# A hybrid encoder layer on one core: the scan's diagonal products with x stationary, and a step planner with other costs

## The chip, the cores and the metric

The kernel runs on one core of a Trainium2 chip, in one launch. The metric is the device time of an execution in microseconds (us). Its engines are named as in the profile: PE (TensorE, the matmuls), PEld (its weight loads), DVE (VectorE), ACT (ScalarE), POOL (GpSimd) and SP (SyncE, whose queue issues the transfers). A matmul has a stationary operand, loaded into the array, and a moving one, streamed through it. [...]

## The reference

One encoder layer is applied to two sequences, 1024 and 256 tokens long, with the same weights: `x + W_out @ concat(scan, window attention, memory attention)(RMSNorm(x))`. The scan group has 16 heads of 64 channels in two groups of eight, chunks of 128 tokens, and runs in both directions over the sequence. What matters here is the part inside a chunk:

```python
seg = acs[:, :, :, None] - acs[:, :, None, :]
decay = jnp.exp(jnp.where(tril, seg, -jnp.inf))
cb = jnp.einsum('bcign,bcjgn->bcijg', Cm, Bm)
y_diag = jnp.einsum('bcijgr,bcjgrp->bcigrp', cb[..., None] * decay, xdt)
...
y = (y_f + y_b + d_skip[:, None] * xs).reshape(b, T, SSD_WIDTH)
```

For each chunk and head, `y_diag` is a product of a 128x128 matrix of weights (positions against positions) with the chunk's 128x64 values. Everything is f32.

## The kernel before, in words

The 1280 tokens are ten blocks of 128. The kernel works in f32 accuracy by splitting each operand of the large projections into a high and a low part in the one-pass type f32r and doing three products. The names: `wh`, `wl` are the weights' parts (made by ACT and DVE from the loaded `wraw`), `xH`, `xL` those of the rows, `acc` the PSUM tiles of the projections (five banks). All other work uses the pool `mix`, three PSUM banks.

The first 740 us of the program and the last 350 are projections with little beside them. In between, the projections to keys, queries, gates and the first half of the output go on, and the scan and both attentions run beside them in four lanes (`ATT`, `SSD`, `PREP`, `DEC`). Each lane is a queue of generators. A generator yields in front of each small step and says with `wants(tiles, banks, after)` which tiles the step needs, how many PSUM banks of `mix` it will open, and which other steps must have been written. `pump`, called after each group of three projection products of a block, gives each lane credit and takes the first lane, in a fixed order, whose next step `may` go.

Whether it may is decided by `Clocks`, a planner that runs while the program is written and not on the chip. It holds a time for each engine, a time at which each tile is full and one at which it is free. `Clocks.cost` estimates an instruction (in ns, `n` elements a partition), `Clocks.ran` moves the clocks on, and `Clocks.ready` compares a step's wants with PE's clock. So an estimate that is off moves a step in each engine's order. On the chip every engine then works through its own order and waits at an instruction whose input is not there. Transfers all go through SP's queue.

The steps around the change are in `decay(t)`, in the lane `DEC`, for each block `t`. Letters stand for them: `R` loads rows of cumulative decay (`rf` and `rb`, by DMA from `ac`), `E` adds a bias on ACT, `C` chooses between the directions on DVE, `D` takes exponentials on ACT, `W` multiplies by `cb` on DVE, which gives the weights `mt` (in the tile `rb`). `Y`, the function `diag(g)`, forms the eight products of group `g` into the bank `py`: the stationary operand is `mt` of one head, 128 columns, and the moving one is that head's 64 columns of `x` (the tile `xs`). DVE then multiplies `x` by the skip and diagonal coefficients into `sk`, adds it to `ya`, adds `py`, and SP stores `ya`. There are 20 such sets, two for each block, with 160 products.

Other names that appear below: `po`, the value products of the window attention (64 columns of `v_all` stationary, two key heads side by side in the output's partitions); `pr`, the four transposes that turn the scan's normalised rows; `psc`, `nm`, `lg` and `ppt`, the window attention's scores, their maxima, their exponentials and the turning of these; `qss`, `qr` and `q`, the norm of the queries (a sum of squares on DVE, a power on POOL, a multiply on DVE); `pmt`, `mpT`, `pmq`, `mqh`, `pms` and `moT`, tiles of the memory attention; `pst`, the scan's state; `xc`, `pxs`, the scan's channels and their turning; `pcb`, the products that give `cb`.

Of the kernel before, what the change touches and what calls it, by code (L numbers as in the profile page):

```python
# [10 lines left out]
F32 = mybir.dt.float32  # L11
# [4 lines left out]
AF = mybir.ActivationFunctionType  # L16
# [3 lines left out]
P = 128  # L20
# [10 lines left out]

RATES = {'kv': (4, 4), 'mq0': (8, 8), 'z0': (8, 8), 'z1': (8, 8), 'mq1': (8, 8), 'o': (8, 8)}
DEBT = 6.0
AHEAD, QUEUE = 300.0, 4000.0
NEG = -1e30

UNITS = (0, 4, 1, 5, 2, 6, 7, 3, 8, 9)
# [5 lines left out]
class Clocks:  # L43
# [17 lines left out]
    def cost(self, e, ins, ops, power):  # L61
        n = max([self.size(x) for x in ops] or [1])
        if e == "PE":
            m = self.size(ops[0])
            one_pass = ops[-1].dtype == F32R or ops[1].dtype == F32R
            return m / 2.4 + 14 if one_pass else max(m / 0.6, 213) + 6
        if e == "DVE":
            return 150 + 1.05 * n
        if e == "ACT":
            return (190 + 0.8 * n if n > 16 else 190) + (190 if len(ins.outs) > 1 else 0)  # L70
        if e == "POOL":
            return 60 + 4.2 * n if n > 16 else 250 + 180 * n if power else 300
        return 50

    def ran(self, e, ins, power=False):
        outs, srcs = [[x.bass_ap for x in xs if hasattr(x, "bass_ap")] for xs in (ins.outs, ins.ins)]
        cost = self.cost(e, ins, outs + srcs, power)
        if e != "SP":
            self.now[e] = max(self.now[e], self.now["PE"])
        if not self.lane:  # L80
            self.now[e] += cost
            return
        at = self.now[e] if e != "SP" else self.now["PE"]
        for x in srcs:
            at = max(at, self.full.get(self.name(x), 0.0))
        for x in outs:
            at = max(at, self.free.get(self.name(x), 0.0))
        if e == "SP":
            end = at + 2600 + self.size(outs[0]) * 1.5
        else:  # L90
            end = self.now[e] = at + cost + 20
        for x in srcs:
            k = self.name(x)
            self.free[k] = max(self.free.get(k, 0.0), end)
        for x in outs:
            k = self.name(x)
            if e != "SP":
                self.free[k] = max(self.free.get(k, 0.0), end)
            self.full[k] = end + 90
# [10 lines left out]

    def ready(self, want):
        tiles, n = want[:2]
        at = [self.full.get(self.name(x), 0.0) - (0 if n else AHEAD) for x in tiles]
        at += [self.opens("mix", 3, i + 1) - 400 * i for i in range(n)]
        at += [self.now[e] - QUEUE for e in ("ACT", "DVE")]
        return max(at) <= self.now["PE"]

# [28 lines left out]
def wants(*tiles, banks=0, after=()):  # L146
    return tiles, banks, after
# [3 lines left out]
def hymba_encoder_kernel(  # L151
# [8 lines left out]
    V, A, G, T, S = [Timed(clk, n, e) for n, e in (("DVE", nc.vector), ("ACT", nc.scalar), ("POOL", nc.gpsimd),  # L160
                                                  ("PE", nc.tensor), ("SP", nc.sync))]
# [18 lines left out]
    fin = early.enter_context(tc.tile_pool(name="early", bufs=1))  # L180
    acc = ctx.enter_context(tc.tile_pool(name="acc", bufs=5, space=bass.MemoryType.PSUM))
    mix = ctx.enter_context(tc.tile_pool(name="mix", bufs=3, space=bass.MemoryType.PSUM))
# [5 lines left out]
    def const(shape, name, dtype=F32):  # L188
        return cp.tile(shape, dtype, tag=name, name=name)
# [4 lines left out]
    def psum(name):  # L194
        return mix.tile([P, 512], F32, tag="mix", name=name)
# [3 lines left out]
    ident = identr.bitcast(F32)  # L199
# [9 lines left out]


    rx = const([P, 14], "rx")
    rbc = const([P, 640], "rbc")
    gq = const([P, 64], "gq")
    dskip, sinkb, dtb, aneg = const([P, 16], "dskip"), const([P, 8], "sinkb"), const([P, 32], "dtb"), const([P, 32], "aneg")
    nsink, pow8 = const([P, 8], "nsink"), const([P, 8], "pow8")
    for h in range(8):
        G.memset(pow8[:, h:h + 1], 2.0 ** (h + 1))
    carry = fin.tile([P, 12, 4], F32, tag="carry", name="carry")
    def dram(shape, name):
        return dr.tile(shape, F32, tag=name, name=name)  # L220
# [32 lines left out]
    ATT, SSD, PREP, DEC = range(4)  # L253
    wanted = [None] * 4
    turn = [0]
    said = set()
# [40 lines left out]
    def may(i):  # L297
        w = wanted[i]
        return owed[i] >= 1 and lanes[i] and (w is None or (said.issuperset(w[2]) and clk.ready(w)))

    def pump(rates):

        for i in range(4):
            owed[i] = min(owed[i] + rates[i % 2], DEBT) if lanes[i] else 0.0
        while True:
            i = next((j for j in (ATT, PREP, SSD, DEC) if may(j)), None)
            if i is None:
                return
            owed[i] -= 1
            step(i)  # L310
# [631 lines left out]
    xs_of, cb_of, dco_of, ya_of = {}, {}, {}, {}  # L942
# [113 lines left out]
    def decay(t):  # L1056
# [4 lines left out]
        def rows(q):  # L1061

            rf = mp.tile([P, 512], F32, tag="rf", name="rf", bufs=2)
            mt = mp.tile([P, 512], F32, tag="rb", name="rb", bufs=RBB)
            r0 = 32 * (t % 5) + 4 * q
            for d, r in enumerate((rf, mt)):
                S.dma_start(r, ac_d[t // 5][r0 + 16 * d:r0 + 16 * d + 4, :]
                            .rearrange("h c -> (h c)").partition_broadcast(P))
            rows_[q] = rf, mt
# [25 lines left out]
        def diag(g):  # L1095
            py = psum("py")
            x, a = xs_of[t][g], ya_of[t, g]
            for h in range(8):
                mt = mts[2 * g + h // 4]
                T.matmul(py[:, h * 64:h * 64 + 64], mt[:, (h % 4) * P:(h % 4 + 1) * P],  # L1100
                         x[:, h * 64:h * 64 + 64], start=True, stop=True)
            sk = a if first else mp.tile([P, 512], F32, tag="rf", name="sk", bufs=2)
            V.tensor_mul(hv(sk), hv(x), hb(dco_of[t][:, 8 * g:8 * g + 8], 8, 64))
            if not first:
                V.tensor_add(a, a, sk)
            V.tensor_add(a, a, py)
            S.dma_start(yp_d[t][:, g * 512:(g + 1) * 512], a)

        rows(0)
        rows(1)  # L1110
        cbs = (("ssd_one", t, "cb"),)
        for what, q in [(x[0], int(x[1])) for x in "E0 C0 E1 D0 R2 C1 W0 D1 E2 W1 C2 Y0 R3 D2 E3 W2 C3 D3 W3".split()]:
            if what == "R":
                rows(q)
            elif what == "E":
                yield wants(rows_[q][0])
                expo(q)
            elif what == "C":
                yield wants(*rows_[q])
                choose(q)  # L1120
            elif what == "D":
                yield wants(rows_[q][1])
                decays(q)
            elif what == "W":
                yield wants(rows_[q][1], after=cbs)
                weights(q)
            else:
                yield wants(mts[1], mts[0], banks=1, after=(("ssd_one", t, 0),))
                diag(0)
        said.add(("decay", t, "weighed"))  # L1130
        yield wants(mts[3], banks=1, after=(("ssd_one", t, 1),))
        diag(1)


    last_y = {}
# [123 lines left out]
    for k in range(8):  # L1259
        at = 2 * k - 5 if k < 4 else 4 * k - 13 if k < 7 else 13  # L1260
# [612 lines left out]
```

## Time and profile before

| | us |
|---|---|
| median of 3 runs | 1775.78 |
| lowest and highest | 1773.38, 1777.44 |
| the profiled execution | 1773.83 |
| its span in the trace | 1772.1 |

The profile is of that one execution. Its rows of matmuls give a start and a duration, and durations of successive matmuls overlap, so that the cost of one in a stream is the distance between starts. An f32 product is recorded as two matmuls, a transpose or an f32r product as one; a few records may be missing. In a row of the timeline stand the start, the duration of the group in us, engine, line, operation, output <- inputs, the stationary shape as rows*columns, the output's shape and the number of records, and in brackets the idle time of that engine just before and what ended it. In a row of the waits stand who waited, for whom, the total in us, how often, and the longest.

### The profile page before, as it was taken

Reading aid. Unit: us, or ns where it says so; the run is one execution under the profiler, and the core shown is the slowest. Engines: PE = TensorE matmul, PEld = TensorE weight load, DVE = VectorE, ACT = ScalarE, POOL = GpSimd, SP = SyncE. Lnnn points to the kernel's source line nnn. Section 1 sums busy time; section 2 is a strip of 40 time slices with the busy share of each in tenths; the row PEclk is TensorE's granted clock in tenths of the full one; section 3 lists DMA queues with packets and bytes.
Section 4 is the critical chain, followed back from the end, with each engine's and each line's share of the span. In section 5 each row is a group of like instructions: output and inputs, shape, how many; then the busy total and the mean of one; then the engine's idle time right before and its main releaser. Section 6 shows DMA issues by size and latency. Waiting matters only on the chain.

```text
span 1772.1 us, 30974 instructions
## 1 busy us (share of the span) xinstructions
PE 1755.3 (99%) x10306; PEld 1572.0 (89%) x10306; DVE 1310.9 (74%) x2417; ACT 971.8 (55%) x2181; POOL 683.8 (39%) x1092
## 2 busy tenths in 40 slices
PE   9999999999999999999999999999999999999999
PEld 7889999999899999988788877887788888889999
DVE  5596788989968888797777877678776533766665
ACT  6554555445545444346787666658886532433332
POOL 0026798860478989220110000111200100068775
PEclk9999999999999999999999999999999999999999
DMA  8794454446544333376467766767785734644442
GB/s 293 238 319 175 136 149 148 128 143 194 156 119 145 119 104 106 90 216 208 143 188 249 259 213 192 226 190 230 243 249 161 222 110 147 207 142 147 145 144 77
DMA packets 210993, 313.23 MB, mean 177 GB/s; under 512 B 21584, under 2 KB 84368, under 8 KB 210832
## 3 DMA queue, kind: packets, MB, share of 16 engines
q1 hardware_dynamic: 210688, 311.19, 56.7%
q8 instruction: 81, 1.33, 0.3%
q14 instruction: 80, 0.66, 0.1%
q10 hardware_dynamic: 144, 0.06, 0.0%
HBM read 242.42 MB, written 68.75 MB: 176 GB/s over the span
## 4 chain that ended last, share of the span: by engine, by line
PE 88%; DMA 4%; DVE 3%; ACT 2%; issue 1%; POOL 1%; SPq 0%; ACTq 0%; DVEq 0%; POOLq 0%
PE acc L128 66%; PE accm L128 11%; PE py L128 2%; PE po L128 1%; PE psc L128 1%; PE pst L128 1%; PE pmo L128 1%; PE pms L128 1%; PE ppt L128 1%; DMA wraw<-in_w_in_laid_dram 1%; PE pyf L128 1%; DMA xst<-in_x_prompt_dram 1%; DVE wl L128 1%; PE pyb L128 0%; ACT lg L128 0%
## 5 line engine op out<-in xcount | busy, mean ns | idle before, releaser
L128 PE MATMUL acc<-wh,xH 128*128 128x512 f32 (+1 forms) x1248 | 490.0, 393 | 0.1
L128 DVE TENSOR_TENSOR wl<-wraw,wh 128x512 fp32r<-128x512 f32 (+1 forms) x480 | 355.5, 744 | 172.9 <-ACT wh L128 170.1
L128 PE MATMUL acc<-wl,xH 128*128 128x512 f32 (+1 forms) x1248 | 473.7, 380 | 0.7 <-DVE wl L128 0.5
L128 PE MATMUL acc<-wh,xL 128*128 128x512 f32 (+1 forms) x1248 | 472.1, 378 | 0.0
L128 ACT ACTIVATE wh<-wraw 128x512 fp32r<-128x512 f32 (+1 forms) x480 | 291.5, 613 | 211.6 <-PE acc L128 136.5
L128 POOL TENSOR_TENSOR ws<-wraw 128x128 f32<-128x128 f32 x224 | 156.9, 700 | 365.8 <-DMA wraw<-in_w_in_pairs_dram 163.1
L128 PEld LDWEIGHTS acc<-wl,xH 128*128 128x128 f32 x1248 | 234.7, 188 | 45.1 <-issue 6.5
L128 PEld LDWEIGHTS acc<-wh,xH 128*128 128x128 f32 x1248 | 234.6, 188 | 44.9 <-issue 7.0
L128 PEld LDWEIGHTS acc<-wh,xL 128*128 128x128 f32 x1248 | 234.2, 188 | 44.6 <-issue 1.0
L128 ACT ACTIVATE sh<-ws 128x384 fp32r<-128x384 f32 x224 | 115.5, 522 | 253.3 <-POOL ws L128 126.6
L128 DVE TENSOR_TENSOR sl<-ws,sh 128x384 fp32r<-128x384 f32 x224 | 158.7, 712 | 115.4 <-ACT sh L128 113.9
L128 POOL TENSOR_TENSOR ws<-wraw,ws 128x128 f32<-128x128 f32 x224 | 153.1, 683 | 17.2
L128 POOL TENSOR_TENSOR ws<-ws,wraw 128x128 f32<-128x128 f32 x224 | 154.3, 689 | 0.0
L128 POOL TENSOR_TENSOR wraw<-wraw 128x128 f32<-128x128 f32 x224 | 139.8, 624 | 17.1
L128 PE MATMUL acc<-xH,wl 128*128 128x320 f32 x320 | 100.0, 312 | 1.0 <-DVE wl L128 1.0
L128 PE MATMUL acc<-tH,sl 128*128 128x320 f32 x320 | 98.9, 309 | 0.0
L128 PE MATMUL acc<-xL,wh 128*128 128x320 f32 x320 | 98.9, 309 | 0.0
L128 PE MATMUL accm<-tH,wl 128*128 128x320 f32 x320 | 98.8, 309 | 0.0
L128 PE MATMUL acc<-tH,sh 128*128 128x320 f32 x320 | 98.7, 309 | 0.0
L128 PE MATMUL acc<-xH,wh 128*128 128x320 f32 x320 | 98.7, 309 | 0.0
L128 PE MATMUL accm<-tL,wh 128*128 128x320 f32 x320 | 98.5, 308 | 0.0
L128 PE MATMUL accm<-tH,wh 128*128 128x320 f32 x320 | 98.5, 308 | 0.0
(458 smaller groups left out, 3829.1 us busy)
## 6 DMA issues: line engine op xcount, KB each, us to landing
wraw<-in_w_in_pairs_dram SPq DMA_DIRECT2D x160, 256.0 KB, 2.7
wraw<-in_w_in_laid_dram SPq DMA_DIRECT2D x128, 256.0 KB, 3.6
wraw<-in_w_out_laid_dram SPq DMA_DIRECT2D x64, 256.0 KB, 3.1
wraw<-in_w_out_pairs_dram SPq DMA_DIRECT2D x64, 256.0 KB, 2.9
rf<-ac SPq DMA_DIRECT2D x40, 256.0 KB, 3.8
rb<-ac SPq DMA_DIRECT2D x40, 256.0 KB, 4.2
wraw<-in_w_mem_laid_dram SPq DMA_DIRECT2D x32, 256.0 KB, 4.7
ra<-in_x_turned_dram SPq DMA_DIRECT2D x16, 320.0 KB, 3.8
```

The costliest lines, as they stand in the source:

```text
L128: r = f(*a, **kw)
```

## The change

Three things change. The diagonal products swap their operands: the 64 columns of `x` of one head are stationary, the weights `mt` are moving, the output has 64 partitions, and an even and an odd head stand side by side in the 128 partitions of `py`, which now holds the result turned. ACT copies it to a new tile `yT`, and a new step `T`, the function `back(g)`, turns it with four transposes into a second bank `pyt`, from which DVE adds. The planner's costs and rules change: estimates for all engines, a latency after ACT and DVE (`LATE`), a margin for tiles that a PE step needs and for banks in place of a fixed advance of 300 ns, and another order of the lanes from the last memory attention of the first half until the sixth block of the scan's second pass. And the row `rbc` of the norm's factors moves to the pool that is given back before the lanes begin.

```diff
-AHEAD, QUEUE = 300.0, 4000.0
+MARGIN, QUEUE = {"PE": 700.0, "bank": 300.0, "other": 0.0}, 4000.0
+LATE = {"ACT": 110.0, "DVE": 90.0}
...
-            return m / 2.4 + 14 if one_pass else max(m / 0.6, 213) + 6
+            return max(m / 2.4 + 14, 85) if one_pass else max(m / 0.6, 213) * list(ops[0].ap)[0][1] / 128 + 6
         if e == "DVE":
-            return 150 + 1.05 * n
+            return 67 + 1.04 * n
         if e == "ACT":
-            return (190 + 0.8 * n if n > 16 else 190) + (190 if len(ins.outs) > 1 else 0)
+            aps = sum(hasattr(x, "bass_ap") for x in ins.ins)
+            return (50 if ops[-aps].space == "PSUM" else 92) + 0.835 * n + 92 * (aps - 1) + (92 if len(ins.outs) > 1 else 0)
         if e == "POOL":
             return 60 + 4.2 * n if n > 16 else 250 + 180 * n if power else 300
...
-            end = self.now[e] = at + cost + 20
+            self.now[e] = at + cost
+            end = at + cost + LATE.get(e, 20)
...
-        at = [self.full.get(self.name(x), 0.0) - (0 if n else AHEAD) for x in tiles]
-        at += [self.opens("mix", 3, i + 1) - 400 * i for i in range(n)]
+        at = [self.full.get(self.name(x), 0.0) + MARGIN["PE" if n else "other"] for x in tiles]
+        at += [self.opens("mix", 3, i + 1) - 400 * i + MARGIN["bank"] for i in range(n)]
...
-    rbc = const([P, 640], "rbc")
+    rbc = fin.tile([P, 640], F32, tag="rbc", name="rbc")
...
-            i = next((j for j in (ATT, PREP, SSD, DEC) if may(j)), None)
+            late = ("mem_attn", 4) in said and ("ssd_two", 5) not in said
+            i = next((j for j in ((SSD, DEC, ATT, PREP) if late else (ATT, PREP, SSD, DEC)) if may(j)), None)
...
                 mt = mts[2 * g + h // 4]
-                T.matmul(py[:, h * 64:h * 64 + 64], mt[:, (h % 4) * P:(h % 4 + 1) * P],
-                         x[:, h * 64:h * 64 + 64], start=True, stop=True)
+                o = h % 2 * 64
+                T.matmul(py[o:o + 64, h // 2 * P:(h // 2 + 1) * P], x[:, h * 64:h * 64 + 64],
+                         mt[:, (h % 4) * P:(h % 4 + 1) * P], start=True, stop=True)
+            yT = mp.tile([P, 512], F32, tag="yT", name="yT", bufs=1)
+            A.activation(yT, py, AF.Copy)
+            yT_.append(yT)
+
+        def back(g):
+            x, a = xs_of[t][g], ya_of[t, g]
+            yT = yT_.pop()
+            py = psum("pyt")
+            for j in range(4):
+                T.transpose(py[:, j * P:(j + 1) * P], yT[:, j * P:(j + 1) * P], ident)
             sk = a if first else mp.tile([P, 512], F32, tag="rf", name="sk", bufs=2)
...
-        for what, q in [(x[0], int(x[1])) for x in "E0 C0 E1 D0 R2 C1 W0 D1 E2 W1 C2 Y0 R3 D2 E3 W2 C3 D3 W3".split()]:
+        for what, q in [(x[0], int(x[1])) for x in "E0 C0 E1 D0 R2 C1 W0 D1 E2 W1 C2 Y0 R3 D2 E3 T0 W2 C3 D3 W3".split()]:
...
         diag(1)
+        yield wants(yT_[0], banks=1)
+        back(1)
```

How the order on the engines moves is shown at three places. The first is PE at the first set of diagonal products, of the last block of the long sequence. Before:

```order
L128 MATMUL acc<-wh,xH_5674 128x512
L128 MATMUL acc<-wl,xH_5674 128x512
L128 MATMUL acc<-wh,xL_5675 128x512
L128 MATMUL py<-xs,rb 128x64 x8
L128 MATMUL acc<-wh,xH_5674 128x512
L128 MATMUL acc<-wl,xH_5674 128x512
L128 MATMUL acc<-wh,xL_5675 128x512
```

And now, from the products on:

```order
L131 MATMUL py<-rb,xs 64x128 x8
L131 MATMUL acc<-wh,xH_5580 128x512
L131 MATMUL acc<-wl,xH_5580 128x512
L131 MATMUL acc<-wh,xL_5581 128x512
L131 MATMUL acc<-wh,xH_5580 128x512
L131 MATMUL acc<-wl,xH_5580 128x512
L131 MATMUL acc<-wh,xL_5581 128x512
```

The products have 64 output partitions and 128 columns in place of 128 and 64, and stand 18 projection products earlier; their transposes `pyt` follow 15 projection products later.

The second is PE at the twelfth set, in the third block from the front of the long sequence. Before:

```order
L128 MATMUL pst<-bh,bth 128x512
L128 MATMUL pst<-bl,bth 128x512
L128 MATMUL pst<-bh,btl 128x512
L128 MATMUL acc<-wh,xH_12222 128x512
L128 MATMUL acc<-wl,xH_12222 128x512
L128 MATMUL acc<-wh,xL_12223 128x512
L128 MATMUL py<-xs,rb 128x64 x8
L128 MATMUL ppt<-identr,lg 128x128 x6
```

And now:

```order
L131 MATMUL pcb<-bc 128x128
L131 MATMUL pcb<-identr,bc 128x128
L131 MATMUL py<-rb,xs 64x128 x8
L131 MATMUL pmt<-identr,mpr 128x128 x4
L131 MATMUL acc<-wh,xH_12729 128x512
L131 MATMUL acc<-wl,xH_12729 128x512
L131 MATMUL acc<-wh,xL_12730 128x512
L131 MATMUL pyt<-identr,yT 128x128 x4
L131 MATMUL pxs<-identr,xc 128x128 x8
```

Here the transposes follow the products closely, behind the turning of the memory attention's weights and three projection products.

The third is DVE at the queries of the second block, where its multiply waits for POOL's power. Before:

```order
L128 TENSOR_REDUCE qss<-sq 128x8
L128 ISA lg,nm<-psc,ndist,nsink 128x256
L128 ISA nm 128x1
L128 TENSOR_TENSOR wl<-wraw,wh 128x512
L128 TENSOR_TENSOR q<-q,qr 128x512
L128 COPY_PREDICATED rb<-upper,rf 128x512
L128 TENSOR_TENSOR qh<-q,qh 128x4x64
L128 ISA lg,nm<-psc,ndist,nsink 128x256
```

And now:

```order
L131 COPY_PREDICATED rb<-upper,rf 128x512
L131 TENSOR_REDUCE qss<-sq 128x8
L131 TENSOR_TENSOR wl<-wraw,wh 128x512
L131 TENSOR_TENSOR q<-q,qr 128x512
L131 ISA lg,nm<-psc,ndist,nsink 128x256
L131 ISA nm 128x1
```

Between the sum of squares and the multiply stood a score step of two instructions and a split; now only the split stands there.

More of the change, by code (lines that the diff above doesn't have):

```diff
@@ L1107, in diag @@
             S.dma_start(yp_d[t][:, g * 512:(g + 1) * 512], a)
+        yT_ = []
         rows(0)
@@ L1132, in decay @@
         diag(1)
+        yield wants(yT_[0], banks=1)
+        back(1)
     last_y = {}
```

4 lines of the change are left out of this document (3 added, 1 removed).

## The prediction

> **What bounds the kernel now.** I read the head of the page first, then the chain of waits.
>
> ```profile
> span 1772.1 us, 30974 instructions
> PE 1755.3 (99%) x10306; PEld 1572.0 (89%) x10306; DVE 1310.9 (74%) x2417; ACT 971.8 (55%) x2181; POOL 683.8 (39%) x1092
> PE 88%; DMA 4%; DVE 3%; ACT 2%; issue 1%; POOL 1%; SPq 0%; ACTq 0%; DVEq 0%; POOLq 0%
> ```
>
> TensorE sets the end: 99% busy, and 88% of the chain. So there are two ways to gain, less work on PE or less of the 1% in which it waits. Busy time is no measure of the first, because each record's duration has a tail that lies over the next record. I therefore read starts from the timeline. For the second, the busy time by stretch, over the part in which the scan and the attention run beside the projections:
>
> ```profile
> core 0: us, PE busy (x) PEld busy (x) DVE busy (x) ACT busy (x) POOL busy (x), PEclk, DMA share, GB/s
> 740.00:800.00 60.00, 58.84 (x344) 51.55 (x343) 52.27 (x130) 27.24 (x63) 9.67 (x16) 1.00 0.63 184
> 800.00:950.00 150.00, 147.94 (x808) 121.22 (x808) 118.62 (x274) 111.15 (x316) 17.91 (x32) 1.00 0.61 190
> 950.00:1100.00 150.00, 146.53 (x802) 118.17 (x799) 112.00 (x244) 102.98 (x275) 11.55 (x21) 1.00 0.70 223
> 1100.00:1250.00 150.00, 148.20 (x813) 120.28 (x812) 113.97 (x249) 102.38 (x261) 22.23 (x45) 1.00 0.71 224
> 1250.00:1420.00 170.00, 168.70 (x939) 137.32 (x938) 114.04 (x258) 118.76 (x321) 19.10 (x40) 1.00 0.70 213
> ```
>
> Of these 680 us PE is busy for 670.2: it waits for 9.8 us, and the clock is full throughout. DVE is busy for 511 us of them (75%), ACT for 463 (68%). The waits one by one, the longest first:
>
> ```profile
> PE py L128 <- ACT mpT L128: 2.3, 1, 2.3
> PE ppt L128 <- DVE nm L128: 1.4, 1, 1.4
> PE po L128 <- ACT pT L128: 0.9, 1, 0.9
> PE pms L128 <- DVE mql L128: 0.9, 1, 0.9
> PE pxs L128 <- DMA xc<-xbc_d: 0.8, 1, 0.8
> ```
>
> The change hardly touches what lies outside this stretch: up to the turned memory keys, at its start, PE's order is the same, and so it is again once the scan and the attention have drained.
>
> **The products.** What one set of eight diagonal products costs now, in starts on PE:
>
> ```profile
> 816.56 0.39 PE L128 MATMUL acc<-wl,xH 128*128 128x512 f32 x1
> 816.78 0.39 PE L128 MATMUL acc<-wh,xL 128*128 128x512 f32 x1
> 817.01 1.89 PE L128 MATMUL py<-xs,rb 128*128 128x64 f32 x16
> 818.71 0.48 PE L128 MATMUL acc<-wh,xH 128*128 128x512 f32 x1
> 819.03 0.39 PE L128 MATMUL acc<-wl,xH 128*128 128x512 f32 x1
> ```
>
> From 816.78 to 819.03 are 2.25 us, in which two projection products go at 0.23 us each: the set costs 2.25 - 0.46 = 1.79 us, 0.22 a product (two records each). After the change the output has 64 partitions, and two heads use the two column halves of the array. The only rows of that form are the value products of the window attention (128*64):
>
> ```profile
> 882.91 0.40 PE L128 MATMUL acc<-wh,xL 128*128 128x512 f32 x1
> 883.24 1.08 PE L128 MATMUL po<-pT,v_all 128*64 128x256 f32 x8
> 884.25 0.87 PE L128 MATMUL pq<-identr,qh 128*128 128x128 f32 x8
> ...
> 918.93 0.39 PE L128 MATMUL acc<-wh,xL 128*128 128x512 f32 x1
> 919.25 1.52 PE L128 MATMUL po<-pT,v_all 128*64 128x256 f32 x12
> 920.69 0.50 PE L128 MATMUL pst<-bh,bth 128*128 128x512 f32 x1
> 921.03 0.40 PE L128 MATMUL pst<-bl,bth 128*128 128x512 f32 x1
> ```
>
> A run of 8 records takes 1.01 us to the next start, a run of 12 takes 1.44: two products more cost 0.43, so 0.215 each at 256 moving columns. The run of six, from 918.93 to 921.03, takes 2.10 - 0.46 = 1.64; without 6 x 0.215 = 1.29 there remain 0.35 us that each run pays for going into the halves and out again. [...]
>
> At 128 moving columns half of 0.215 is 0.108. A weight load could be slower than that:
>
> ```profile
> L128 PEld LDWEIGHTS py<-xs,rb x320: 186/192/192, 816.8 to 1372.1; 128*128 128x128 f32 x160
> L128 PEld LDWEIGHTS po<-pT,v_all x208: 132/137/137, 873.2 to 1366.1; 128*64 128x64 f32 x104
> ```
>
> 64 columns fewer take 55 ns less, so two loads of 64 keep a product at about 0.11. I take 0.11. The lower end is 0.108 with only the 0.15 us inside the run paid (1.01 - 4 x 0.215); the upper end is a load that is not hidden, 0.11 + 0.055 = 0.165. A set then costs 8 x 0.11 + 0.35 = 1.23 us (1.01 to 1.67). With 160 products by the row above there are 20 sets: 20 x (1.23 - 1.79) = -11.2 us (-15.6 to -2.4).
>
> **The turning back** adds to each set four transposes, for which the ones of the normalised rows stand:
>
> ```profile
> 1169.39 0.39 PE L128 MATMUL acc<-wh,xL 128*128 128x512 f32 x1
> 1169.62 0.60 PE L128 MATMUL pr<-identr,yd 128*128 128x128 f32 x4
> 1169.97 0.48 PE L128 MATMUL acc<-wh,xH 128*128 128x512 f32 x1
> 1170.29 0.40 PE L128 MATMUL acc<-wl,xH 128*128 128x512 f32 x1
> ```
>
> 0.90 - 0.46 = 0.44 us, so 20 x 0.44 = +8.8 us. **On PE the two nearly cancel: -2.4 us** (-6.8 to +6.4). The products have to stay under 0.125 us each to gain anything: (1.79 - 0.35 - 0.44) / 8.
>
> The copy out of PSUM is new on ACT, 20 times 128x512. Its duration, and its spacing to the next of its size:
>
> ```profile
> 1094.79 0.57 ACT L128 ACTIVATE mpT<-pmt 128x512 f32<-128x512 f32 x1
> 1095.27 0.57 ACT L128 ACTIVATE mqh<-pmq 128x512 fp32r<-128x512 f32 x1
> ```
>
> 0.48 us each, 9.6 us in all on an engine that is idle for 217 of the 680: it costs nothing as long as the transposes behind it do not come too early. The new order puts them behind at least three projection products and other work. DVE does what it did, with its last addition reading the transposes' bank in place of the products'. Each set now needs a bank of the three twice. The move of the row of norms into the early pool frees the space of the new tile and issues nothing.
>
> **The estimates.** The step planner decides where PE's small work stands, and a wait arises where it believes an input ready that is not. Two of them, in their rows:
>
> ```profile
> 863.68 2.12 POOL L128 TENSOR_TENSOR qr<-qr,mhalf 128x8 f32<-128x8 f32 x1
> 866.12 0.69 DVE L128 TENSOR_TENSOR q<-q,qr 128x512 f32<-128x512 f32 x1 [1.81 <-POOL qr L128]
> 868.23 0.44 PE L128 MATMUL ppt<-identr,lg 128*128 128x128 f32 x2 [1.39 <-DVE nm L128]
> 1091.91 1.28 ACT L128 ACTIVATE rf<-rf,wj_all 128x128 f32<-128x128 f32 x4 [4.16 <-DMA rf<-ac]
> 1095.41 1.77 PE L128 MATMUL py<-xs,rb 128*128 128x64 f32 x14 [2.25 <-ACT mpT L128]
> ```
>
> In the first, DVE sits for 1.81 us behind a power on POOL that lasted 2.12 (estimate 0.25 + 8 x 0.18 = 1.69, unchanged by the diff). In the second, ACT sits for 4.16 us behind a row load, and what PE needs is queued behind it. Load estimates are unchanged too. So neither is cured at its root: the 0.8 us on the load of xc and the 2.3 us stay, and of the 1.4 us some go. The rest of the 9.8 us, some 5, are waits of 0.2 to 0.9 us behind DVE and ACT, about nine of them. For these the new rule asks that the input be ready 0.7 us before PE is there, and a bank 0.3 us. Against that, the old costs were too high, and this was a margin too: 0.60 us for a 128x512 copy out of PSUM, where the rows above show 0.48. One error went the other way. The value products were charged 256/0.6 + 6 = 433 ns, where the rows show 215, so each run of four or six put the planner's PE clock 0.9 to 1.3 us too far on and made everything behind it look ready. I take 0.4 us off nine waits: -3.5 us. The ends are -7 (all but the loads) and +3 (a new wait like the second).
>
> **Sum.** The profiled execution took 1773.83 us, its span 1772.1. 1773.83 - 2.4 - 3.5 = 1767.9. The median of the runs shown, 1775.78, is 1.95 above that execution, so the forecast is 1769.9 us.
>
> **Rivals.**
> *The waits move, they do not go.* For: in DVE's new order only one split stands between the sum of squares and the multiply that waits for POOL's power, where three instructions stood. Against: the 0.7 us is wider than most of those waits. Only PE's -2.4 remains: 1773.4 us.
> *The halves do not pay.* One mechanism: each record of 128 columns waits for its load of 64, at 0.165 us a product in each of the 20 sets. For: no row shows loads every 55 ns, since the value products load every 0.108 us. Against: they hide them fully. From 0.125 us on, PE loses. At 0.165 it loses 6.4, with -3.5 from the waits: 1778.7 us, slower.
> *The copies choke ACT.* A set's products shrink by 0.56 us on PE, and a 0.48 us copy is added on an engine that is 68% busy and works in order. If PE waited 0.4 us for it in each of the 20 sets, that would be +8.0, and 1777.9 us. I count it with the case above, as slower. [...]
> [...]
> That the change does not do what it says is hardly possible: the products stand in the new form in the order.
>
> **How the numbers follow.** Forecast 0.50, waits move 0.20, slower by loads 0.06 and by copies 0.07, more goes 0.15, and 0.02 for what I do not see. The likeliest case's own range is 1766 to 1773. The range reaches down into the fourth case and up to where the slower ones begin, 1763 to 1778; half of these three, and the rest, lie outside. About 0.2%, 3.6 us, is what a measurement of this kernel can tell from no change. Faster by more: nearly nine tenths of the forecast, all of "more goes", a little of "waits move", together 0.63. Within: 0.22. Slower: 0.15.
>
> **What would show it.** Right: the products as 128*64 with 128 columns, a set of 16 records about 1.0 us to the next start (now 1.70), four transposes at 0.44, PE's wait in the same stretch near 6 us. Wrong in the first term: more than 1.2 us to the next start. Wrong in the second: 9 us of waits or more, or a row of the turned products waiting for ACT's copy. The whole is wrong if the 2.3 us wait behind a row load multiplies, since one such load takes back what the products give.

## The result, and the profile after

| | before | after |
|---|---|---|
| median of 15 runs each | 1776.78 us | 1780.41 us |
| lowest and highest | 1773.38, 1781.04 | 1777.63, 1783.78 |
| ratio of after to before, 95% interval | | 1.0020 [1.0012, 1.0028] |
| the profiled execution, its span | 1773.83, 1772.1 | 1781.58, 1779.9 |

The change makes the kernel 0.2% slower, 3.6 us between the medians. The two profiled executions lie 7.75 us apart, because that of before is 2.95 us under its median and that of after 1.17 above. So the traces tell where time went, and overstate how much.

The head of the page of after, and its chain of waits:

```profile
span 1779.9 us, 31164 instructions
PE 1754.5 (99%) x10386; PEld 1560.6 (88%) x10386; DVE 1309.1 (74%) x2417; ACT 981.8 (55%) x2201; POOL 684.6 (38%) x1092
PE 77%; DMA 7%; DVE 5%; POOL 5%; ACT 3%; issue 3%; SPq 0%; DVEq 0%; POOLq 0%; ACTq 0%
```

PE's busy time is 0.8 us below before's; its share of the chain fell from 88 to 77%. The busy time by stretch says where it waits:

```profile
core 0: us, PE busy (x) PEld busy (x) DVE busy (x) ACT busy (x) POOL busy (x), PEclk, DMA share, GB/s
740.00:800.00 60.00, 57.44 (x349) 51.51 (x348) 50.57 (x129) 28.38 (x63) 9.52 (x16) 1.00 0.62 185
800.00:950.00 150.00, 145.42 (x820) 115.61 (x819) 113.82 (x272) 111.60 (x310) 16.76 (x32) 1.00 0.58 176
950.00:1100.00 150.00, 145.97 (x824) 115.71 (x823) 108.81 (x238) 104.11 (x280) 10.91 (x21) 1.00 0.73 226
1100.00:1250.00 150.00, 148.32 (x834) 119.23 (x834) 114.60 (x246) 106.03 (x269) 23.39 (x41) 1.00 0.66 207
1250.00:1420.00 170.00, 166.70 (x930) 131.86 (x930) 116.08 (x260) 117.87 (x321) 20.59 (x39) 1.00 0.72 224
sum 680.00, PE 663.86 PEld 533.92 DVE 503.89 ACT 467.99 POOL 81.16; mean PE 132.77 PEld 106.78 DVE 100.78 ACT 93.60 POOL 16.23
```

PE waits for 680 - 663.86 = 16.1 us in this part of the program, where it waited for 9.8. Over the whole span, adding up the gaps in PE's records, it is 20.3 us against 11.8; the largest single part of what was added outside the stretch is one more wait of 1.1 us, of `pms` behind ACT's `so`, at 1438 us.

The products and their turning went as costed. PE's timeline at the first set and at a run of transposes that stands by itself:

```profile
816.24 0.39 PE L131 MATMUL acc<-wh,xL 128*128 128x512 f32 x1
816.56 1.09 PE L131 MATMUL py<-rb,xs 128*64 128x128 f32 x16
817.58 0.50 PE L131 MATMUL acc<-wh,xH 128*128 128x512 f32 x1
817.92 0.40 PE L131 MATMUL acc<-wl,xH 128*128 128x512 f32 x1
...
1118.14 0.40 PE L131 MATMUL pst<-fh,btl 128*128 128x512 f32 x1
1118.37 0.63 PE L131 MATMUL pyt<-identr,yT 128*128 128x128 f32 x4
1118.76 0.48 PE L131 MATMUL acc<-wh,xH 128*128 128x512 f32 x1
1119.08 0.39 PE L131 MATMUL acc<-wl,xH 128*128 128x512 f32 x1
```

The set of 16 records takes 1.02 us to the next start, and 1.68 - 0.46 = 1.22 us with the way in and out (1.23 predicted). The transposes cost 0.94 - 0.46 = 0.48 (0.44 predicted).

What PE waits for is new. Its waits in this stretch whose tile is `psc`, the window attention's scores, before and after:

```profile
PE psc L128 <- ACT st L128: 0.5, 1, 0.5
PE psc L128 <- ACT pT L128: 0.2, 1, 0.2
PE psc L128 <- ACT kL L128: 0.2, 1, 0.2
```

```profile
PE psc L131 <- DVE nm L131: 1.9, 2, 1.2
PE psc L131 <- DVE ya L131: 1.3, 2, 0.7
PE psc L131 <- DVE state L131: 1.2, 1, 1.2
PE psc L131 <- ACT so L131: 1.1, 1, 1.1
PE psc L131 <- DVE moT L131: 0.9, 1, 0.9
PE psc L131 <- ACT qT L131: 0.8, 1, 0.8
PE psc L131 <- ACT pT L131: 0.8, 1, 0.8
PE psc L131 <- ACT cb L131: 0.7, 1, 0.7
```

These are 8.7 us, 0.9 before. A score product reads only `kT`, `kL` and `qT`; but for `qT` the instructions named here read one of the three banks of `mix` (PSUM tiles of 128x512 f32) and so give it back, or (`nm`) stand directly behind the one that does. The scores are only a part of it. All waits above 0.15 us in which PE was about to write a bank of `mix`, and the releaser that the trace names had read one (`nm` counts with these) and gave PE no input, are 5.9 us before and 11.7 after: of the 6.3 us that PE's waits rose by, 5.8 are for banks. Two waits that are not for banks are longer or new: 1.2 us of `acc` behind `wl` at 761 us, where before has 0.5, and 1.4 us of `pmk` at 766 us. They stand in e3, p4, e5, b1, b2 and b3 below as well. One of the waits for a bank, followed back in the timeline of ACT and PE:

```profile
1309.18 1.28 ACT L131 ACTIVATE rf<-rf,wj_all 128x128 f32<-128x128 f32 x4 [1.23 <-DMA rf<-ac]
1310.37 0.49 ACT L131 ACTIVATE lg<-lg,nm 128x256 f32<-128x256 f32 x1
...
1311.45 0.61 ACT L131 ACTIVATE wh<-wraw 128x512 fp32r<-128x512 f32 x1
1311.96 0.57 ACT L131 ACTIVATE so<-pr 128x512 f32<-128x512 f32 x1
...
1312.59 0.39 PE L131 MATMUL psc<-kT,qT 128*128 128x256 f32 x1 [1.09 <-ACT so L131]
```

ACT sits for 1.23 us behind the load of `rf`. The copy `so<-pr`, which empties a bank, is queued behind it, and PE wants that bank. It is the same kind of wait as before's 2.3 us at 1095.41, only that no single one is long; there are 18 waits above 0.15 us in place of 13.

### The profile page after: what moved, and what is told of

Read it like the earlier page. It is cut to its first block, busy times and chain, and to the rows that moved or that the text cites. A ratio compares the mean times of both kernels' runs of the same rounds, so it can differ in the third digit from the quotient of the medians.

```text
span 1779.9 us, 31164 instructions
## 1 busy us (share of the span) xinstructions
PE 1754.5 (99%) x10386; PEld 1560.6 (88%) x10386; DVE 1309.1 (74%) x2417; ACT 981.8 (55%) x2201; POOL 684.6 (38%) x1092
## 4 chain that ended last, share of the span: by engine, by line
PE 77%; DMA 7%; DVE 5%; POOL 5%; ACT 3%; issue 3%; SPq 0%; DVEq 0%; POOLq 0%; ACTq 0%
PE acc L131 59%; PE accm L131 8%; POOL ws L131 3%; DMA rb<-ac 1%; PE psc L131 1%; PE po L131 1%; DVE wl L131 1%; DMA rf<-ac 1%; DMA wraw<-in_w_in_pairs_dram 1%; POOL wraw L131 1%; PE ppt L131 1%; PE pst L131 1%; PE pmo L131 1%; DMA sst<-in_x_sample_dram 1%; PE py L131 1%
## 5 line engine op out<-in xcount | busy, mean ns | idle before, releaser
L131 POOL TENSOR_TENSOR ws<-wraw 128x128 f32<-128x128 f32 x224 | 152.5, 681 | 340.7 <-ACT rH L131 119.3
L131 POOL TENSOR_TENSOR ws<-wraw,ws 128x128 f32<-128x128 f32 x224 | 154.5, 690 | 17.2
```

What stands on the lines that cost most here:

```text
L131: r = f(*a, **kw)
```

## The experiments

Two theories stood at the start. **The work:** the sum of products and transposes is wrong somewhere. **The order:** PE's work is as costed, and the waits belong to the new order of the engines (theory 1 in the expectations, which puts the loss on the planner). The second then split: before's order waits unusually little, and nearly any other order of its planner waits more (theory 2 in the later expectations); a margin for banks of about 1 us removes the waits (theory 3); the planner's short estimate of loads is the root (theory 4). All ratios are to runs of the kernel before on the same chip in the same job, whose median was 1776.2 to 1776.8 us.

### The work alone

e1, the kernel before with the operands swapped and neither the copy nor the turning back, so that DVE adds turned products and the output is another one:

```diff
-                T.matmul(py[:, h * 64:h * 64 + 64], mt[:, (h % 4) * P:(h % 4 + 1) * P],
-                         x[:, h * 64:h * 64 + 64], start=True, stop=True)
+                o = h % 2 * 64
+                T.matmul(py[o:o + 64, h // 2 * P:(h // 2 + 1) * P], x[:, h * 64:h * 64 + 64],
+                         mt[:, (h % 4) * P:(h % 4 + 1) * P], start=True, stop=True)
```

> The kernel before with only the operands of the diagonal products swapped; nothing copies or turns the result back, so DVE adds the turned products (that part of the computation is left out). Each engine's order is that of the kernel before. Theory 1 (the products' work on PE is as costed, the waits ate it): 0.56 us less in each of 20 sets, so 11 us faster than before (9 to 13), waits of PE between 740 and 1420 us as before, near 10 us. Rival (the swap itself costs PE time that starts do not show): 0 to 5 us faster.

e2, the whole change of the products (copy, turning back, `rbc`), with the planner of before; the diff is against the changed kernel:

```diff
-MARGIN, QUEUE = {"PE": 700.0, "bank": 300.0, "other": 0.0}, 4000.0
-LATE = {"ACT": 110.0, "DVE": 90.0}
+AHEAD, QUEUE = 300.0, 4000.0
...
-        at = [self.full.get(self.name(x), 0.0) + MARGIN["PE" if n else "other"] for x in tiles]
-        at += [self.opens("mix", 3, i + 1) - 400 * i + MARGIN["bank"] for i in range(n)]
+        at = [self.full.get(self.name(x), 0.0) - (0 if n else AHEAD) for x in tiles]
+        at += [self.opens("mix", 3, i + 1) - 400 * i for i in range(n)]
...
```

> The whole change of the products (swap, copy, turning back, the norm's row moved) with the planner of before: its costs, its rules, its lane order. Theory 1 (work on PE -2.4 us, the loss comes from the planner): 2.4 us faster than before, within 3. Rival (the copy and the second bank make the waits, whatever the planner): 3 to 6 us slower, with rows of PE waiting for the copy or for banks of 3 us in all or more.

Their busy times, from the heads of the pages of e1 and of e2:

```profile
PE 1743.9 (99%) x10306; PEld 1551.4 (88%) x10306; DVE 1308.8 (74%) x2417; ACT 970.1 (55%) x2181; POOL 685.2 (39%) x1092
```

```profile
PE 1753.4 (99%) x10386; PEld 1559.1 (88%) x10386; DVE 1312.1 (74%) x2417; ACT 980.8 (55%) x2201; POOL 681.1 (38%) x1092
```

e1 took 1768.2 us, ratio 0.9957 [0.9944, 0.9969]. PE is busy for 11.4 us less than before; the prediction had 11.2. e2 is busy for 9.5 us more than e1; the prediction had 8.8 for the transposes. (Busy is here the time in which any record of PE runs; with the gaps it makes up PE's share of the span, so that the tails that overlap are not counted twice.) The work theory falls: both terms are right to 0.7 us. But e1 gained 8 us, which lies in neither of the two ranges expected, and e2 took 1779.88 us, 1.0019 [1.0010, 1.0027]: it is slower with less work and the old planner, by as much as the rival expected. PE's gaps sum to 17.2 us in e1 and 18.1 in e2, 11.8 before. So it isn't the new planner alone that brings waits.

Two kinds can be read from the traces. e1's order on PE differs from before's in a dozen rows only, and its waits stand mostly where before's do; some are longer. A row of before, and two of e1 (for `xc` before's was 0.8):

```profile
PE pms L128 <- DVE moT L128: 0.6, 1, 0.6
```

```profile
PE pms L128 <- DVE moT L128: 2.7, 1, 2.7
PE pxs L128 <- DMA xc<-xbc_d: 2.7, 4, 1.0
```

PE comes sooner, and DVE and the loads not by as much: a part of the saving turns into waiting, with hardly a change of order. In e2, PE waits for the copy, as the rival said:

```profile
PE pyt L128 <- ACT yT L128: 2.3, 2, 1.2
```

### The planner alone

e3 is the reverse of e2, the changed planner with the products of before; e4 is the changed kernel with the old cost lines of DVE and ACT and without `LATE`. From e4's diff:

```diff
-            return 67 + 1.04 * n
+            return 150 + 1.05 * n
...
-            self.now[e] = at + cost
-            end = at + cost + LATE.get(e, 20)
+            end = self.now[e] = at + cost + 20
```

> The changed planner (costs, margins, lane order) and the moved norm's row, with the diagonal products as before. Theory 1 (the planner makes the loss): 5 to 7 us slower than before, PE waiting 15 us or more between 740 and 1420 us, most of it at the attention's scores for a bank. Rival (the loss is the products'): within 2 us of before, waits near 10 us or below.

> The changed kernel with one piece of the planner as before: the estimates of DVE and ACT and what is added to an instruction's end. Theory 1 in its narrow form (the old overcharge of DVE and ACT was the margin that covered their waits for DMA and POOL, and the true costs took it away): PE's waits between 740 and 1420 us fall from 16 to 8 or below, and the time is 5 to 8 us below the changed kernel, 2 to 4 below the kernel before. Rival (the margin rules or the lane order make the waits): within 2 us of the changed kernel.

e3 took 1783.66 us, 1.0037 [1.0024, 1.0051], with gaps of 18.8 us, and e4 1778.22, 1.0006 [0.9997, 1.0015], with 15.5. The new planner costs 0.37% with the old products, though not where it was expected: only 1.6 us of e3's waits are at the scores. e4's waits between 740 and 1420 us are 12.6 us and not 8 or below, so the overcharge of DVE and ACT is not the whole cause either. In e4's order it does act as a margin for banks: by the count used above, e4 waits 3.9 us for banks where after waits 11.7, and more for other things. With the new products, either planner gives about the same time (after 1.0020, e2 1.0019). No single part is to blame: each combination but that of before waits for 15 to 20 us. The margins and the order of the lanes were not put back one by one.

### Is before's order a good draw?

If so, any small push to its planner must cost time. p2 and p3 change one number each in the kernel before, p4 one in the changed kernel:

```diff
-AHEAD, QUEUE = 300.0, 4000.0
+AHEAD, QUEUE = 330.0, 4000.0
```

> The kernel before with one number of the planner moved by a trifle: the advance of a step without a bank 330 ns in place of 300. No instruction is added or removed, only PE's order in the middle of the program shifts. Theory 2 (the order of the kernel before happens to fit the chip, and nearly any other order that this planner gives waits 4 to 6 us more, whatever moved it): 3 to 7 us slower than before, PE's idle time near 17 us where it was 12. Rival (the products' copy and banks, or the margins, make the waits): within 1.5 us of before.

```diff
-            return 150 + 1.05 * n
+            return 148 + 1.05 * n
```

> The kernel before with another trifle: a DVE instruction's fixed estimate 148 ns in place of 150. Theory 2 as for the advance of 330: 3 to 7 us slower than before, and not the same waits as there. Rival: within 1.5 us of before.

```diff
-MARGIN, QUEUE = {"PE": 700.0, "bank": 300.0, "other": 0.0}, 4000.0
+MARGIN, QUEUE = {"PE": 720.0, "bank": 300.0, "other": 0.0}, 4000.0
```

> The changed kernel with its margin for a PE step 720 ns in place of 700, which shifts its order as much as a trifle does the order before. Theory 2 (the changed kernel's order is one draw among many, near their middle): within 3 us of the changed kernel, to either side, with other waits. Rival (its waits have one cause in the change): within 1 us of the changed kernel and the same kinds of waits, most at the attention's scores for a bank.

p2 took 1783.98 us, 1.0037 [1.0025, 1.0049], and p3 1780.2, 1.0020 [1.0009, 1.0030]. Neither changes any work, and 2 ns in the estimate of a DVE instruction cost as much as the whole change under study. p4 took 1782.16, 1.0033 [1.0020, 1.0045], and waits elsewhere than after does. Its longest wait, in ACT's and PE's rows:

```profile
1035.38 0.63 ACT L131 ACTIVATE sq<-mq 128x512 f32<-128x512 f32 x1 [3.90 <-DMA mq<-mq]
...
1038.38 0.36 ACT L131 ACTIVATE cb<-pcb 128x256 f32<-128x256 f32 x1
...
1038.80 1.98 PE L131 MATMUL py<-rb,xs 128*64 128x128 f32 x16 [4.41 <-ACT cb L131]
```

ACT stands for 3.9 us behind a load of `mq` and, in between, for 1.3 us behind one of `rf`, and the emptying of a bank (`cb<-pcb`) is queued behind both. Theory 2 is borne out: p3 and p4 lie where it put them, p2 just above.

### The margin for banks

Since the waits of after are for banks, e5 asks that a bank be free 1.0 us ahead, in place of 0.3; b1 and b2 try the numbers beside it, b3 is e5 with the products of before, b4 is e5 with the margin for tiles doubled too.

```diff
-MARGIN, QUEUE = {"PE": 700.0, "bank": 300.0, "other": 0.0}, 4000.0
+MARGIN, QUEUE = {"PE": 700.0, "bank": 1000.0, "other": 0.0}, 4000.0
```

> The changed kernel with a margin for a bank of 1000 ns in place of 300. If the waits at the attention's scores come from a bank that the planner believes free too early, they fall from some 8 us to 3 or below, and the time falls by 3 to 6 us against the changed kernel. Theory 2 (any order waits some 17 us, for something else each time): those at the scores fall and others come, the time stays within 2.5 us of the changed kernel.

> The changed kernel with a margin for a bank of 1100 ns. Against the run with 1000 ns its order differs in some 740 rows. Theory 3 (a margin of about 1 us for a bank really takes waits away): within 2.5 us of the run with 1000 ns, so 1772 to 1777 us, 0 to 5 us below the kernel before. Theory 2 (that run was one lucky order among many): 1777 to 1784 us, PE's idle time 16 us or more.

> The same with 900 ns. Theory 3: 1772 to 1777 us. Theory 2: 1777 to 1784 us.

> The changed planner with a margin for a bank of 1000 ns, and the diagonal products as in the kernel before. Theory 1 (the products save 2.4 us on PE, under any planner): slower than the same planner with the changed products by 1 to 5 us, the spread of two orders included, and PE busy for 1.5 to 3 us more where the clock is full in both. Rival (the products cost more than they save, as the first comparison seemed to say): 2 us or more faster than it.

> The changed kernel with a margin of 1400 ns for a PE step's tiles and 1000 ns for a bank. Theory 3 carried on (the waits come from DVE and ACT being held by loads and by POOL for 0.5 to 4 us, which no estimate knows, so a wider margin takes more of them away): PE's idle time below 13 us, 1768 to 1774 us. Theory 2: 1777 to 1784 us. If the lanes come too late instead, their work is pushed together at the end of the stage and idle time appears after 1420 us.

e5 took 1774.19 us, 0.9982 [0.9973, 0.9990]; b1 1774.58, 0.9988 [0.9979, 0.9997]; b2 1774.28, 0.9984 [0.9975, 0.9992]. Three different orders end within 0.4 us, so this isn't a draw of one, and all three beat both kernels, the kernel before by 0.1 to 0.2%. b2's waits for `psc`:

```profile
PE psc L131 <- ACT pT L131: 0.5, 2, 0.4
PE psc L131 <- DVE ya L131: 0.3, 1, 0.3
PE psc L131 <- DVE nm L131: 0.2, 1, 0.2
```

They fell from 8.7 us to 1.0. Waits for banks as a whole did not vanish: they are 5.0 to 6.2 us in these three, where after has 11.7, and b2's longest wait, 2.1 us, is one. b4, with the same margin for banks as e5 and a wider one for tiles, took 1777.97 us, 1.0005 [0.9995, 1.0015]: 3.8 us more than e5, where theory 3 carried on expected less, and inside theory 2's range. So the draw of the order still counts for a few us. And b3 took 1790.72, 1.0071 [1.0055, 1.0086]: with the old products the same margin does not help; it is some 16 us slower than e5, where 1 to 5 were expected of the products. Its longest wait:

```profile
988.22 0.69 ACT L131 ACTIVATE rf<-rf,wj_all 128x128 f32<-128x128 f32 x2 [4.52 <-DMA rf<-ac]
...
990.92 0.84 ACT L131 ACTIVATE pT<-ppt 128x384 f32<-128x384 f32 x2
...
991.44 0.69 PE L131 MATMUL psc<-kT,qT 128*128 128x384 f32 x1 [3.28 <-ACT pT L131]
```

### The load estimate

Behind the waits of after, p4 and b3 that are followed back above stands a load that came later than the planner thought: from issue to landing, the one of `rf` in after took 5.1 us, that of `mq` in p4 4.6 and that of `rf` in b3 7.8, where the planner has 2.6 + 512 x 0.0015 = 3.4. So the estimate was raised, in the kernel before (l1), in the changed kernel (l2), in e5 (l3) and in b3 (l4):

```diff
-            end = at + 2600 + self.size(outs[0]) * 1.5
+            end = at + 3400 + self.size(outs[0]) * 1.5
```

> The kernel before; only the planner's estimate of a load goes from 2.6 to 3.4 us (plus 1.5 ns an element, unchanged), so a row set of 512 elements is expected after 4.2 us, which is what the traces show for rf and rb (3.8 to 4.6 us from issue to landing). If the short load estimate is what makes waits in new orders (theory 4), this new order has no wait on PE above 1.5 us, PE idles 8 to 11 us of the span (11.8 in before's trace), and the time is 1772 to 1776 us. If before's own order is just a good draw and any other order of its planner is worse by the two margins measured so far (theory 2, +3.4 and +7.2 us), it idles 13 to 17 us and takes 1779 to 1785 us.

> The changed kernel with the load estimate 3.4 us in place of 2.6. Theory 4: the rows of ACT and DVE that wait more than 2 us behind rf<-ac and rb<-ac no longer stand ahead of what PE needs; PE idles 9 to 12 us (20 in the changed kernel's profiled run), no window at half clock, 1768 to 1773 us. Theory 2 (another draw): idle 13 to 21 us, 1774 to 1782 us. PE's busy time is 1752 to 1755 in either.

> The changed kernel with the bank margin of 1.0 us (measured: 1774.2) and the load estimate of 3.4 us. Theory 4: what is left of the waits there (14.1 us idle) falls to 9 to 11, 1769 to 1772 us. Theory 3 (the bank margin alone removes what can be removed): 1773 to 1775 us. Theory 2: 1774 to 1782 us.

> The changed planner with the bank margin of 1.0 us and the load estimate of 3.4 us, but the diagonal products of the kernel before (no copy, no turning back). With l3 this is a pair that differs in the products alone, as the changed kernel and its own pair do. Theory 4: the 23.1 us idle of the pair at 2.6 us, which its trace puts behind a 4.5 us wait for rf<-ac, fall to 10 to 13; 1774 to 1778 us, so the products' change is worth 3 to 6 us at equal waits. Theory 2: idle anywhere from 13 to 23 us, 1779 to 1791 us.

l1 took 1788.24 us, 1.0064 [1.0051, 1.0078]; l2 1780.51, 1.0023 [1.0014, 1.0032]; l3 1774.52, 0.9985 [0.9977, 0.9994]; l4 1781.3, 1.0028 [1.0019, 1.0038]. Theory 4 falls, as far as it was tried: 3.4 us gives 4.2 for such a load, still less than those three took, and a longer estimate was not run. The longer estimate made the kernel before 12 us slower, beyond both ranges expected, and left after and e5 where they were; only b3 gained, 9 us, and stayed 3 above what was expected of it. In l1 the long wait has only moved on to another load:

```profile
1222.34 0.63 ACT L128 ACTIVATE sq<-q 128x512 f32<-128x512 f32 x1 [3.15 <-DMA q<-q]
1223.00 0.69 DVE L128 TENSOR_REDUCE qss<-sq 128x8 f32<-128x512 f32 x1 [2.66 <-ACT sq L128]
...
1224.07 1.67 PE L128 MATMUL pyb<-state,cc 128*128 128x512 f32 x2 [2.94 <-DVE moT L128]
```

l2 and l3 differ in the margin for banks alone, as after and e5 do. Their waits for `psc`, of l2 and of l3:

```profile
PE psc L131 <- ACT pT L131: 5.4, 6, 1.6
PE psc L131 <- ACT cb L131: 2.7, 1, 2.7
```

```profile
PE psc L131 <- ACT pT L131: 1.3, 2, 0.7
```

8.1 us of waits became 1.3, and the time fell by 6.0 us. With after and e5 that is a second pair of orders in which the margin takes the waits at the scores away, and about half of all waits for banks (12.1 to 5.5 us, and 11.7 to 5.3). For the new products theory 3 holds; with the old ones it does not.

### All orders together

PE's gaps are summed over the span of each profiled execution; `psc` is the part of them in front of scores, from 740 to 1420 us (a sum of rounded rows), and `banks` the part that was for a bank of `mix`, counted as above in the same stretch. e1, which leaves the turning back out, is not in the table.

| kernel | products | median us | ratio | PE busy | gaps | psc | banks |
|---|---|---|---|---|---|---|---|
| before | old | 1776.8 | 1 | 1755.3 | 11.8 | 0.9 | 5.9 |
| p2, ahead 330 | old | 1784.0 | 1.0037 | 1761.8 | 16.5 | 1.8 | 7.3 |
| p3, DVE 148 | old | 1780.2 | 1.0020 | 1759.7 | 13.7 | 4.4 | 5.5 |
| l1, load 3400 | old | 1788.2 | 1.0064 | 1763.6 | 19.1 | 2.7 | 13.5 |
| e3, new planner | old | 1783.7 | 1.0037 | 1759.9 | 18.8 | 1.6 | 6.8 |
| b3, its bank 1000 | old | 1790.7 | 1.0071 | 1761.7 | 23.1 | 7.7 | 12.7 |
| l4, and load 3400 | old | 1781.3 | 1.0028 | 1757.4 | 15.8 | 3.2 | 9.9 |
| e2, old planner | new | 1779.9 | 1.0019 | 1753.4 | 18.1 | 3.2 | 6.3 |
| after | new | 1780.4 | 1.0020 | 1754.5 | 20.3 | 8.7 | 11.7 |
| e4, old ACT, DVE costs | new | 1778.2 | 1.0006 | 1757.9 | 15.5 | 2.9 | 3.9 |
| p4, tiles 720 | new | 1782.2 | 1.0033 | 1754.4 | 20.6 | 2.5 | 14.6 |
| l2, load 3400 | new | 1780.5 | 1.0023 | 1755.0 | 18.4 | 8.1 | 12.1 |
| b2, bank 900 | new | 1774.3 | 0.9984 | 1753.1 | 12.6 | 1.0 | 6.2 |
| e5, bank 1000 | new | 1774.2 | 0.9982 | 1753.6 | 14.1 | 2.9 | 5.3 |
| b1, bank 1100 | new | 1774.6 | 0.9988 | 1753.4 | 13.3 | 1.8 | 5.0 |
| l3, bank 1000, load 3400 | new | 1774.5 | 0.9985 | 1754.3 | 14.7 | 1.3 | 5.5 |
| b4, bank 1000, tiles 1400 | new | 1778.0 | 1.0005 | 1755.2 | 15.7 | 2.2 | 4.3 |

Before has the smallest gaps of all. The six other orders with the old products take 1780.2 to 1790.7 us, 1784.7 on average; the ten with the new ones 1774.2 to 1782.2, 1777.7 on average. Four pairs differ in the products alone. With the new products the time goes by +0.2% (e2 to before), -0.2% (after to e3), -0.9% (e5 to b3) and -0.4% (l3 to l4). So the products' change is worth having in every pair but the one whose old side is the order of before. How much of that is the products' own can't be read from four pairs: PE's work differs by some 2 us, each pair's two orders differ as well, and the averages mix margins. Without the wider margin for banks, the five new ones (e2, after, e4, p4, l2) take 1780.2 us on average and the four old ones besides before (p2, p3, l1, e3) 1784.0.

The last column bears theory 3 out beyond the scores: among the orders of the new planner and new products with its own costs, those with 0.3 us (after, p4, l2) wait 11.7 to 14.6 us for banks, the five with 0.9 to 1.1 us 4.3 to 6.2. With the old products there is no such division: b3 waits 12.7 us with the wider margin, e3 6.8 without. What makes the order of before fit so well was not found; that its numbers had been chosen by their time would explain it, and nothing here shows it.

## Why the prediction was wrong

It said 1769.9 us, 1763 to 1778, and faster with a chance of 0.63; the time is 1780.4, slower by 0.20%, 2.4 us above the range. One us of the distance is the start: three runs of before gave 1775.78, fifteen 1776.78.

- **The products, -11.2 us: right.** e1 shows -11.4, and a set costs 1.22 us. The 0.35 us for going into the halves and out, an estimate read from rows of the value products, held: the products alone, 8 x 0.11 = 0.88 us, would have missed the 1.22.
- **The turning back, +8.8: right,** a little more, 9.5 between e1 and e2.
- **ACT's copy costs nothing: not quite.** In after, PE stands before the transposes twice, 0.9 us for `yT` and 0.8 behind ACT's `kL`; in e2 it waits 2.3 us for `yT`. That is far from the rival's 8.0 us in after, so that this rival is out in the form it was priced; the one of loads that are not hidden is out too.
- **The waits, -3.5 us: the step that failed.** In the two traces they rose by 6.3 us between 740 and 1420 us, 5.8 of them for banks, and by 8.5 over the span. The prediction's own sign for this, 9 us of waits or more, came true with 16.1. "I take 0.4 us off nine waits" treated each of before's waits as an item that stays in its place and gets shorter. But the change gives PE, ACT and DVE another order, in which most of before's waits are gone and others are there. And with PE's own saving a wait that stays can grow, as in e1 the one of `pms` from 0.6 to 2.7 us. What the orders of these planners have, 12.6 to 23.1 us of gaps in sixteen of them, was not known; 11.8 was taken for the usual and is the least. The upper end of this term, "+3 (a new wait like the second)", counted one new wait; the eighteen in after make up nearly all of its 16.1 us.
- **A cost that was named and not priced.** "Each set now needs a bank of the three twice" stands in the prediction without a number. Before's waits for banks, 5.9 us, became 11.7 with a margin of 0.3 us; with 0.9 to 1.1 us they are 4.3 to 6.2. The 0.3 us was read there as a margin that shortens waits, and the old overcharge was named as a margin too but not priced. How much of the rise belongs to the second bank and how much to the planner stays open: neither e2 (6.3 us) nor e3 (6.8) shows it alone, and l1 and b3, with the old products, have 13.5 and 12.7.
- **"The whole is wrong if the 2.3 us wait behind a row load multiplies":** this kind of wait is the one that the traces show, a reader queued on ACT or DVE behind an instruction that waits for a load (ACT for 1.23 us in after, 3.90 in p4, 4.52 in b3). But in after the waits are many short ones, and not all are behind loads; long ones are in p4, b3 and l1.
- Of the rivals, "the waits move, they do not go" names what happened, but its price, 1773.4 us, takes their sum to stay as it is. The others ended on one part that is dearer. None said that the order of before could be better than its planner's orders are in general, though its price, 1784.7 - 1776.8 or some 8 us with the old products, is more than the whole gain that was forecast. No run shows the -4.5 us on PE that goes with the 0.15 for "more goes": PE is busy for 1.9 us less in e2 than in before and for 0.8 less in after, and its waits did not fall by 7 us but rose, in after by 6.3.

## What to carry to other kernels

Where an order comes out of a planner or scheduler, a change of a few us in the work is smaller than what the order itself draws: push the planner of before by a number that means nothing, two or three times, and take the spread of these times (here 3 to 12 us on the planner of before, all upward) as the uncertainty of the forecast, and as the ground on which to compare. The work can be summed from starts in the trace; waits can't be summed from the old trace once the order moves. If a change opens more buffers of a small pool, price that first: here, with the new products, the margin for a free bank made the difference between 0.2% slower and 0.2% faster. And count on a part of what is saved on the busiest engine to come back as waiting for the others: e1 saved 11.4 us and gained 8.

## What the hardware showed that was not expected

After some single waits of PE the granted clock falls to one half for 3.41 us. In p2 it does, and in b2 it does not; the stretch with a wait and the one behind it, each 3.41 us:

```profile
1314.17:1317.58 3.41, 1.57 (x16) 1.34 (x14) 1.70 (x4) 3.41 (x12) 0.19 (x1) 1.00 1.02 375
1317.58:1320.99 3.41, 3.41 (x14) 1.93 (x13) 2.35 (x7) 3.09 (x11) 0.00 (x0) 0.50 0.89 273
```

```profile
1297.64:1301.05 3.41, 1.59 (x9) 1.03 (x7) 2.34 (x4) 1.85 (x4) 0.96 (x2) 1.00 0.79 276
1301.05:1304.46 3.41, 3.17 (x17) 1.81 (x18) 3.41 (x7) 3.02 (x10) 0.00 (x0) 1.00 0.62 153
```

The granted clock is the third number from the end of a row: 0.50 in the second of p2, 1.00 in the second of b2. In each of the 18 traces all changes of the clock, the first and the last of the program among them, fall on one grid of 3.413 us (in before the first and the last lie 517 cells apart, in after 519). On that grid, and leaving out the end of the program, a cell at half clock followed each of the ten cells in which PE was idle for 1.84 us or more, and two more, with 1.68 (p3) and 1.77 (l1); none of those with 1.63 or less was followed by one, nor were three with 1.68 (l2), 1.80 (e1) and 1.82 (b2, above). So in these traces the two kinds of cell part between 1.63 and 1.84 us of idle time, about half a cell, and before's wait of 2.25 us, of which 1.36 lie in one cell and 0.89 in the next, was followed by none: the clock there is 1.00. Twice, in e4 and l1, the half rate lasted for two cells (the mean clock is 0.94 in e4 from 1020 to 1080 us and 0.97 in l1 from 1100 to 1250 us). In e3's cell at half clock, from 1060.25 us on, two projection products start 0.42 us apart in place of 0.23, so by an estimate such a cell costs up to 1.7 us of PE's work, half of 3.41. This may be a part of why p2 and b3, with two such cells each, and l1, where three cells were at half, show 1761.7 us of busy time and more. p4, with two, shows 1754.4, so the cells do not settle the busy time by themselves.
